# Mixer layer: products of the Fourier and pooling branches moved into the gate groups, the convolution's left behind them

## The chip, the cores and the metric

One core of one Trainium2 chip runs one program that holds a recurrent block, a mixture of experts and two dense layers. The metric is the device time of that program in microseconds (us). Three runs gave 2937.89, 2939.16 and 2935.10 us, so the median is 2937.89 us.

## The reference, cut to what matters

The change lies in the mixer of the dense layers, which runs twice (`l` = 0, 1). With `h` of 512 tokens x 1024 features:

```python
p = h @ w_in[l]                                  # 1024 -> 5 x 512 + 3 x 1024
gates = sigmoid(p[..., OFF_G:]).reshape(b, s, 3, 1024)
y_f = fourier_mix(p[..., F], w_fourier[l])       # 4 groups of 128 -> 256 each
y_c = short_conv(p[..., B], p[..., C], p[..., V], w_conv[l], w_conv_out[l])   # 512 -> 1024
y_p = pool_mix(p[..., P], w_pool[l], pool_scale[l])   # 4 groups (windows 2, 4, 8, 16), 128 -> 256 each
merged = gates[:, :, 0] * y_f + gates[:, :, 1] * y_c + gates[:, :, 2] * y_p
x = x + merged @ w_o[l]
```

Everything is float32. Each matrix product is done as three float32r products of split operands: high part x high part, high x low, low x high.

## The kernel before, in words

Features lie on partitions: a tile is 128 features x 512 tokens, and the model's 1024 features are eight tiles `j` = 0 to 7. The helper `mm3` (L237 to L241) issues the three matmuls of a product: L239 with the high parts, L240 with the input's low part, L241 with the weights' low part.

**Weights.** The class `Stream` reads all weights in the order of their use. A block of 128 x 2048 (1 MB) comes in two halves of 1024 columns; ACT makes the high part `whi` of a half (L190) and DVE the low part `wlo` (L191), into a ring of five halves. `advance(h)`, called when PE's matmuls of half `h` have been issued, splits the next half, so that four halves lie ahead, and `_dma` issues loads as soon as a buffer is free in program order. Loads go through SyncE's queue (SP, L156). The buffers are two `raw`, and inside a section of the layer one `rawf` and one `rawg` (half a block).

**Gate groups.** Four output tiles at a time are computed by `group` in seven steps of 24 matmuls of 256 columns each, with sums of weight blocks. For those sums a pair of weight blocks is loaded as three blocks, of which the first and the third (in `rawg`) get a second load that adds (L154), issued by POOL's queue, since it accumulates. DVE adds two more sums (L196). A group so has seven halves of weights. Its results leave PSUM by six DVE operations (L1603 to L1608, L1626) and copies of ACT.

**Jobs.** Beside the groups, work of earlier groups runs as generators (`jobs`). `tick` at the end of each step runs the next piece of each job, before that step's `advance`; `steps(s3=[...])` starts a job in step 3.

The mixer's groups: the Fourier input, then `c0`, the transform over time, `c1`, `b` and `p` (convolution and pooling inputs), then six gate groups `n` = 0 to 5. Before the change these hold the pooling gates of tiles 0 to 3 and 4 to 7, and four groups with the gates of convolution and Fourier for two tiles each (1, 2, 3, 0). `store` (L1786) takes the sigmoid of a group's results on ACT and writes them to DRAM (`keep`, called `gates` in the trace) through SyncE; only the last group's stay on chip. The split branches go to DRAM as well (`aside`, L1713, `branch` in the trace), and `back` (L1804) reads one branch of a group again, high and low half of 256 KB each, through POOL's queue; `load` (L1827) reads a gate. On chip the groups' split inputs hold 28 of the 40 buffers `s`, and the convolution's result `BC` holds 8.

**The tail of the mixer** (L1849 to L1873). For each tile `j`: four products of the convolution, one of the Fourier branch and one of the pooling branch (18 matmuls of 512 columns), then on DVE gate times product (L1860), two more products (L1862, L1864), two sums (L1863, L1865), on ACT the high part of the merged tile (L1867) and on DVE its low part (L1868), which runs in the next tile's `tick`. Two halves of `w_o` are used on the way (`begin`, behind `j` = 4 and 6), the other six behind the loop (`out_part`).

Of the kernel before, what the change touches and what calls it, by code (L numbers as in the profile page):

```python
# [10 lines left out]
F32 = mybir.dt.float32  # L11
F32R = mybir.dt.float32r
# [9 lines left out]
S = 512  # L22
# [11 lines left out]
JO = (0, 4, 1, 5, 2, 6, 3, 7)  # L34

MIX_OUT = [(j, range(4)) for j in JO[:4]] + [(j, range(4, 7)) for j in JO[:4]] + [(j, (7,)) for j in JO[:4]]
MIX_OUT += [(j, range(8)) for j in JO[4:]]
L2 = 2
# [30 lines left out]
MIX = [((0, 2), (1, 3)), ((8, 12), (9, 13)), ((10, 14), (11, 15)), ((4, 6), (5, 7)), ((16, 18), (17, 19))]  # L69
MIX += [((36 + 4 * i, 38 + 4 * i), (37 + 4 * i, 39 + 4 * i)) for i in range(2)]  # L70
MIX += [((28 + 2 * i, 20 + 2 * i), (29 + 2 * i, 21 + 2 * i)) for i in (1, 2, 3, 0)]


class Stream:
# [35 lines left out]
    def add(self, items, keep=()):  # L110


        self.keep = set(keep)
        self.used = set()
        for it in items:
            if not isinstance(it, tuple):
# [12 lines left out]
            self._ent(a, 0, (a, 1))  # L129
            self._ent(c, 0)  # L130
            self._ent(a, 1)
# [31 lines left out]
    def _src(self, b, half):  # L163
        return self.raw[b][:, half * HB:(half + 1) * HB]

# [7 lines left out]
    def _split(self, late=None):  # L173
# [8 lines left out]
        if b in self.keep:  # L182
            self.half[h] = src
            return True
        hi = self.pool.tile([128, HB], F32R, name="whi", tag="whi", bufs=self.nh)
        lo = self.pool.tile([128, HB], F32R, name="wlo", tag="wlo", bufs=self.nh)
        self.half[h] = (hi, lo)
# [56 lines left out]
def build(tc, A):  # L244
    nc = tc.nc
    ctx = ExitStack()
    with ctx:
# [21 lines left out]
        YD = DR_.tile([S * 2, D], F32, name="YD")  # L269
        keep = [DR_.tile([24, 128, S], F32, name=f"gates{l}") for l in range(L2)]  # L270
        keep_s = [DR_.tile([16, 128, S], F32, name=f"branch{l}") for l in range(L2)]
# [984 lines left out]
def dense_phase(K):  # L1256
# [157 lines left out]

    def out_part(x, done, nxt=lambda j: None, tail=None, order=None, ps=None):

        nonlocal h
        n = 0
        ps = ps or {}
        for j, ks in order or out_order(len(x)):  # L1420
            if tail and j == KD - 1:
# [166 lines left out]
    def mixer(l, nxt):  # L1588
# [58 lines left out]

        def split(src):

            hi, lo = slot(), slot()  # L1650
# [57 lines left out]

        def aside(n, src):

            t = yield from split(src)
            for i in range(2):
                nc.sync.dma_start(keep_s[2 * n + i], t[i].bitcast(F32))  # L1713
# [37 lines left out]

        def pool(t, i):
            half = 1 << i
# [19 lines left out]
            yield  # L1773
            yield from aside(4 + i, t)

# [9 lines left out]

        def store(t, f, n, i):  # L1786

# [4 lines left out]
            for r in range(2):  # L1792
                if n < 5:
                    o = 4 * i + r + 16 if n < 2 else 2 * (2 * i + r)
                    d = keep[o:o + 3:2] if n < 2 else keep[o:o + 2]
                    nc.sync.dma_start(d.rearrange("m p x -> p m x"), t[r].rearrange("p (m x) -> p m x", m=2))
                    yield
                else:
                    G[r] = t[r][:, :S], t[r][:, S:]

# [5 lines left out]

        FT, PL, GP = {}, {}, {}
        new = dict(s0=[once(f3)], s1=[pool(p[0], 0)], s4=[pool(p[1], 1)])
        for n, i in enumerate((0, 1, 1, 2, 3, 0)):
            if n == 5:  # L1810
                FT[0], PL[0] = back(0), back(4)
                v = lines()
                for j in range(2):
                    GP[j] = v[:, j, :S]
                    nc.gpsimd.dma_start(GP[j], keep[16 + j])
            t, f = rows(steps(**new))
            new = dict(s0=[store(t, f, n, i)])
            if n == 0:
                new["s0"].append(pool(p[0], 2))
                new["s3"] = [pool(p[1], 3)]  # L1820
        tick(new["s0"])
        tick()
        assert not jobs

        def load(n):
# [3 lines left out]

        M, PO = [], {}  # L1830

        def begin(js):

            nonlocal h
            w = st.get(h)
            for n, j in enumerate(js):
                PO[j] = bank()
                for k in range(4):
                    sl = slice((4 * n + k) * 128, (4 * n + k + 1) * 128)
                    mm3(nc, PO[j], (w[0][:, sl], w[1][:, sl]), M[k], k == 0, False)  # L1840
            st.advance(h)
            h += 1

        for j in range(KD):
            g = j // 2
            if j % 2 == 0 and j + 2 < KD:
                FT[g + 1], PL[g + 1] = back(g + 1), back(5 + g)
                for i in (j + 2, j + 3):
                    G[i] = load(2 * i), load(2 * i + 1)  # L1849
                    GP[i] = load(16 + i)  # L1850
            gc, gf = G[j]
            gp = GP[j]
            w = st.get(h)
# [15 lines left out]
            if j == 4:  # L1869
                begin(JO[:2])  # L1870
            if j == 6:
                begin(JO[2:4])
        tick()  # L1873
# [4 lines left out]
        open_ffn(3 * l + 2)  # L1878
        out_part(M, done, nxt, order=MIX_OUT[4:], ps=PO)

# [97 lines left out]
def layout(I):  # L1978
# [63 lines left out]
    for e in range(NE):  # L2042
# [4 lines left out]
        [np.asarray(I["moe_w_group"])[0], np.asarray(I["moe_w_expert"])[0]], 1).reshape(KD, 128, 36).transpose(1, 0, 2))  # L2047
    A["rbias"] = np.concatenate([np.asarray(I["moe_b_group"])[0], np.asarray(I["moe_b_expert"])[0]])[None]
    for l in range(L2):
        W = {n: np.asarray(I[n + "_2"])[l] for n in ("w1_a", "w3_a", "w2_a", "w_in", "w_fourier", "w_conv_out",  # L2050
# [25 lines left out]
        tco = tiles(W["w_conv_out"])  # L2076
        hv = []
        for j in range(KD):
            g, r = divmod(j, 2)
            sl = slice(128 * r, 128 * r + 128)  # L2080
            misc = np.zeros((128, 8, 128), f)
            misc[:, 0:4] = tco[j]
            misc[:, 4] = W["w_fourier"][g][:, sl]
            misc[:, 5] = W["w_pool"][g][:, sl]
            hv.append(misc)
        t2 = tiles(W["w_o"])
        ho = list(np.stack([t2[j, :, k] for j, ks in MIX_OUT for k in ks])
                  .reshape(-1, 8, 128, 128).transpose(0, 2, 1, 3))
        hv[5:] = ho[:1] + hv[5:7] + ho[1:2] + hv[7:] + ho[2:]
        put(np.stack([np.ascontiguousarray(v).reshape(128, HB) for v in hv]))  # L2090
# [17 lines left out]
    A["edge"] = ed  # L2108
    A["wblocks"] = np.concatenate(blocks)
    return A  # L2110

# [14 lines left out]
```

## Time and profile before

| | |
|---|---|
| median of three runs | 2937.89 us |
| the profiled execution | 2939.49 us, span 2937.3 us |
| busy share of the span | PE 97%, DVE 76%, ACT 57%, POOL 14% |
| chain that ended last | PE 67%, DVE 9%, ACT 4%, DMA 1% |
| HBM | 557.75 MB read, 33.03 MB written |

A row of the chain or of the time order names engine, line, operation and tiles (out<-in). `[1.68 <-DVE L L1864]` behind a row says that the engine was idle for 1.68 us before it and that the DVE operation of line L1864 ended that. PE's matmuls are pipelined: the time from one start to the next is what one costs, not the duration beside it.

### The profile page before, as it was taken

What the parts mean: (1) busy time and instruction counts of PE and PEld (TensorE: products, weight loads), DVE (VectorE), ACT (ScalarE), POOL (GpSimd) and SP (SyncE); (2) the same over time, 40 slices, a digit from 0 to 9 for tenths busy, and PEclk for the clock granted to TensorE, in tenths of its full rate; (3) what the DMA queues carried; (4) which work ended last, traced back from release to release, by engine and by line L of the source; (5) the groups of instructions that cost most, each with busy time, mean ns of one, the idle gap of its engine ahead of it and who ended that gap; (6) DMA issues with size and microseconds to landing.
All of it is one profiled execution on the core that took longest, in us unless ns stands there. A gap on an engine that the chain in (4) does not pass through costs nothing.

```text
span 2937.3 us, 44478 instructions
## 1 busy us (share of the span) xinstructions
PE 2838.0 (97%) x17882; PEld 2466.9 (84%) x17882; DVE 2239.8 (76%) x2778; ACT 1660.6 (57%) x2214; POOL 421.1 (14%) x395
## 2 busy tenths in 40 slices
PE   9997999999889999999989999999999999899998
PEld 7875666667558989899969999899898999699997
DVE  7688888898986858789678667777587896786674
ACT  4756888888764535655536344644356555363443
POOL 0034222220520000100210000100001002100002
PEclk9998999999999999999999999999999999999999
DMA  6374898999943545478944555465464689445552
GB/s 198 124 279 158 336 361 344 370 365 378 351 161 115 144 136 169 126 192 243 290 153 133 160 162 147 130 179 144 137 176 120 194 242 295 148 139 154 162 144 72
DMA packets 118433, 589.72 MB, mean 201 GB/s; under 512 B 13692, under 2 KB 24316, under 8 KB 65360
## 3 DMA queue, kind: packets, MB, share of 16 engines
q1 hardware_dynamic: 90160, 493.70, 46.2%
q0 software_dynamic: 26976, 92.11, 15.3%
q8 instruction: 141, 2.31, 0.3%
q10 hardware_dynamic: 1088, 1.05, 0.1%
q14 instruction: 68, 0.56, 0.1%
HBM read 557.75 MB, written 33.03 MB: 201 GB/s over the span
## 4 chain that ended last, share of the span: by engine, by line
PE 67%; DVE 9%; ACT 4%; issue 2%; DMA 1%; POOL 0%; DVEq 0%; POOLq 0%; ACTq 0%
PE mm L240 12%; PE mm L241 12%; PE mm L239 12%; PE sv L239 8%; PE sv L241 8%; PE sv L240 8%; DVE wlo L191 4%; ACT whi L190 2%; PE y L949 2%; PE h L914 2%; PE h L913 1%; PE ht L927 1%; DMA raw<-in_wblocks 1%; DVE raw L196 1%; PE gat L884 1%
## 5 line engine op out<-in xcount | busy, mean ns | idle before, releaser
L191 DVE TENSOR_TENSOR wlo<-raw,whi 128x1024 fp32r<-128x1024 f32 x501 | 615.1, 1239 | 199.4 <-ACT whi L190 199.0
L240 PE MATMUL mm<-s,whi 128*128 128x256 f32 (+1 forms) x2246 | 734.2, 327 | 9.6 <-DVE s L1868 9.6
L239 PE MATMUL mm<-s,whi 128*128 128x256 f32 (+1 forms) x2246 | 734.1, 327 | 7.5 <-ACT s L1867 5.3
L241 PE MATMUL mm<-s,wlo 128*128 128x256 f32 (+1 forms) x2246 | 733.4, 327 | 0.0
L190 ACT ACTIVATE whi<-raw 128x1024 fp32r<-128x1024 f32 x503 | 520.1, 1050 | 128.8 <-PE mm L240 88.4
L239 PE MATMUL sv<-s,whi 128*128 128x256 f32 (+1 forms) x1928 | 553.0, 287 | 9.6 <-DVE L L1864 4.1
L240 PE MATMUL sv<-s,whi 128*128 128x256 f32 (+1 forms) x1928 | 551.8, 286 | 0.0
L241 PE MATMUL sv<-s,wlo 128*128 128x256 f32 (+1 forms) x1928 | 551.8, 286 | 0.0
L240 PEld LDWEIGHTS mm<-s,whi 128*128 128x128 f32 x2246 | 425.6, 189 | 50.2 <-DVE s L1868 11.5
L239 PEld LDWEIGHTS mm<-s,whi 128*128 128x128 f32 x2246 | 426.0, 190 | 47.2 <-ACT s L1867 6.1
L241 PEld LDWEIGHTS mm<-s,wlo 128*128 128x128 f32 x2246 | 425.7, 190 | 38.1
L239 PEld LDWEIGHTS sv<-s,whi 128*128 128x128 f32 x1928 | 364.5, 189 | 15.5 <-DVE L L1864 5.3
L241 PEld LDWEIGHTS sv<-s,wlo 128*128 128x128 f32 x1928 | 364.5, 189 | 2.9
L240 PEld LDWEIGHTS sv<-s,whi 128*128 128x128 f32 x1928 | 364.3, 189 | 2.6
L191 DVE TENSOR_TENSOR wlo<-rawf,whi 128x1024 fp32r<-128x1024 f32 x158 | 194.3, 1230 | 69.1 <-ACT whi L190 69.1
L191 DVE TENSOR_TENSOR wlo<-rawb,whi 128x1024 fp32r<-128x1024 f32 x162 | 203.7, 1299 | 22.8 <-ACT whi L190 20.5
L1585 DVE SCALAR_TENSOR_TENSOR X<-mm,X 128x512 f32<-128x512 f32 x95 | 65.6, 691 | 188.1 <-PE mm L241 188.1
L190 ACT ACTIVATE whi<-rawf 128x1024 fp32r<-128x1024 f32 x158 | 166.0, 1050 | 69.3 <-PE mm L240 46.7
L914 PE MATMUL h<-wlo,xt 128*64 128x512 f32 x512 | 195.9, 403 | 6.7 <-DVE wlo L191 5.8
L154 POOL DMA_DIRECT2D rawg<-in_wblocks x63 | 54.6, 867 | 944.3 <-DVE wlo L191 512.2
L913 PE MATMUL h<-whi,xt 128*128 128x512 f32 x448 | 181.6, 405 | 6.0 <-PEq L1125 5.2
L949 PE MATMUL y<-whi,hd 128*64 128x512 f32 x512 | 161.7, 397 | 2.5 <-ACT whi L190 1.5
(459 smaller groups left out, 4696.7 us busy)
## 6 DMA issues: line engine op xcount, KB each, us to landing
raw<-in_wblocks SPq DMA_DIRECT2D x201, 1024.0 KB, 5.3
rawb<-in_wblocks SPq DMA_DIRECT2D x81, 1024.0 KB, 6.8
rawf<-in_wblocks SPq DMA_DIRECT2D x64, 1024.0 KB, 5.1
rawa<-in_wblocks SPq DMA_DIRECT2D x57, 1024.0 KB, 6.8
rawg<-in_wblocks SPq DMA_DIRECT2D x63, 512.0 KB, 3.7
rawg<-in_wblocks POOLq DMA_DIRECT2D x63, 512.0 KB, 6.9
raw<-in_wblocks POOLq DMA_DIRECT2D x48, 512.0 KB, 5.6
gates<-T SPq DMA_DIRECT2D x20, 512.0 KB, 6.7
```

The lines of the kernel that those rows point to most:

```text
L154: self.nc.gpsimd.dma_start(t[:, x:y], src, accum_op=OP.add)
L190: self.nc.scalar.activation(hi, src, AF.Copy)
L191: f = lambda E=self.nc.vector: E.tensor_tensor(lo, src, hi, op=OP.subtract)
L196: f = lambda E=self.nc.vector: E.tensor_tensor(t, t, u, op=OP.add)
L239: nc.tensor.matmul(ps, wh, xh, start=first, stop=False, skip_group_check=skip)
L240: nc.tensor.matmul(ps, wh, xl, start=False, stop=False, skip_group_check=skip)
L241: nc.tensor.matmul(ps, wl, xh, start=False, stop=last, skip_group_check=skip)
L884: nc.tensor.matmul(ps[:, 256 * v:256 * v + 256], x[c][:, sl], K["oh", g][0][:, c], start=c == 0, stop=c == 3)
L913: nc.tensor.matmul(ps, x, w[0][:, sl], start=k == 0, stop=False)
L914: nc.tensor.matmul(ps[:64], x[:, 0:64], w[1][:, sl], start=False, stop=False)
L949: nc.tensor.matmul(ps[i][:64], hd[:, f, v:v + 64], w[wv][:, sl], start=f == 0 and n == 0, stop=f == 3 and n == 2)
L1585: STT(X[j], ps, 0.5, X[j], op0=OP.mult, op1=OP.add)
```

## The change

The order of the gate groups, the place of two of three branch products, and the layout of their weights change. What is computed stays.

- Gate group `n` = 0 now has the convolution's gates of tiles 4 to 7 (stored). Groups 1 to 4 have the gates of pooling and Fourier for the two tiles of one branch group `g` = 2, 3, 0, 1. Group 5 has the convolution's gates of tiles 0 to 3 (kept).
- The products of the branches of `g` stand at the end of its gate group: 12 matmuls of 512 columns into four banks, from a narrow weight block (`wbranch`, 128 x 512) that is loaded through SyncE into a buffer of the ring `t`. The branch's halves are read back by POOL in step 3 of the same group.
- During the next group `gates_pf` multiplies gates and products and adds the two (6 DVE operations a group). The sums `Z` of `g` = 0, 1 stay on chip, those of `g` = 2, 3 go to DRAM and are loaded later.
- Pooling 2 and 3 run beside `n` = 0 and 1, pooling 0 beside 1, pooling 1 beside 2.
- The loop behind the groups has the convolution's product, one multiplication and one addition for each tile; its weights come two tiles to a half. `w_o` stands wholly behind the loop, in the order of `out_order`.

```diff
+MIX += [((32, 34), (33, 35))]
+MIX += [((36 + 2 * i, 20 + 2 * i), (37 + 2 * i, 21 + 2 * i)) for i in (2, 3, 0, 1)]
+MIX += [((28, 30), (29, 31))]
...
-            order += b[:2] + [A["dfts"]] + b[2:]
+            order += b[:2] + [A["dfts"]] + b[2:6]
+            for g in (2, 3, 0, 1):
+                order += [b.pop(6), A["wbranch"][l, g]]
+            order += b[6:]
             sects.append((a, count(order)))
-            order += blocks(8)
+            order += blocks(6)
...
+        if i in (1, 4):
+            st.slots_from(p, "t", 1, lo, hi, bufs=NT_F, w=S)
...
+        def gates_pf(t, f, g, ps):
+
+            f()
+            act(t[0], t[0], AF.Sigmoid)
+            yield
+            act(t[1], t[1], AF.Sigmoid)
+            yield
+            for r in range(2):
+                yield
+                j = 2 * g + r
+                u, v = t[r][:, :S], t[r][:, S:]
+                STT(u, ps[2 * r], vc("pscale", KD * l + j), u, op0=OP.mult, op1=OP.mult)
+                TT(v, v, ps[2 * r + 1], op=OP.mult)
+                if g < 2:
+                    if r == 0:
+                        Z["t"] = lines()
+                    Z[j] = Z["t"][:, r, :S]
+                    TT(Z[j], u, v, op=OP.add)
+                else:
+                    z = tmp()
+                    TT(z, u, v, op=OP.add)
+                    nc.sync.dma_start(keep[8 + j], z)
+                yield
...
+        def branches(g):
+            BR[0], BR[1] = back(4 + g), back(g)
...
+        new = dict(s0=[once(f3), pool(p[0], 2)], s3=[pool(p[1], 3)])
+        for n, g in enumerate((4, 2, 3, 0, 1, 5)):
+            if g < 4:
+                new["s3"] = [once(lambda: branches(g))]
+                if n < 3:
+                    new["s1"] = [pool(p[n - 1], n - 1, spare)]
+            if g == 5:
+                loads(4)
+                loads(5)
+            t, f = rows(steps(**new))
+            if g >= 4:
+                new = dict(s0=[gates_c(t, f, 5 - g)])
+                continue
             w = st.get(h)
-            for n, j in enumerate(js):
-                PO[j] = bank()
-                for k in range(4):
...
+            ps = [bank() for _ in range(4)]
+            for i in range(4):
+                sl = slice(128 * i, 128 * i + 128)
+                mm3(nc, ps[i], (w[0][:, sl], w[1][:, sl]), BR[i % 2], True, True)
             st.advance(h)
             h += 1
+            new = dict(s0=[gates_pf(t, f, g, ps)])
...
+        loads(6)
+        loads(7)
+        M = []
         for j in range(KD):
...
-            py, pf, pq = bank(), bank(), sbank()
-            chunk(w, BC, py)
-            mm3(nc, pf, (w[0][:, 512:640], w[1][:, 512:640]), FT[g], True, True)
-            mm3(nc, pq, (w[0][:, 640:768], w[1][:, 640:768]), PL[g], True, True)
-            st.advance(h)
-            h += 1
+            gc = G[j]
+            py = bank()
+            chunk(st.get(h), BC, py, t0=4 * (j % 2))
             TT(gc, gc, py, op=OP.mult)
             tick()
-            TT(gf, gf, pf, op=OP.mult)
-            TT(gc, gc, gf, op=OP.add)
-            STT(gp, pq, vc("pscale", KD * l + j), gp, op0=OP.mult, op1=OP.mult)
-            TT(gc, gc, gp, op=OP.add)
+            TT(gc, gc, Z[j], op=OP.add)
+            if j % 2:
+                st.advance(h)
+                h += 1
...
-        out_part(M, done, nxt, order=MIX_OUT[4:], ps=PO)
+        out_part(M, done, nxt)
```

## Rows read from the trace of the kernel before

**Rows 1.** The page: busy time, chain by engine, a DMA issue (us to landing).

```profile
PE 2838.0 (97%) x17882; PEld 2466.9 (84%) x17882; DVE 2239.8 (76%) x2778; ACT 1660.6 (57%) x2214; POOL 421.1 (14%) x395
...
PE 67%; DVE 9%; ACT 4%; issue 2%; DMA 1%; POOL 0%; DVEq 0%; POOLq 0%; ACTq 0%
...
rawg<-in_wblocks SPq DMA_DIRECT2D x63, 512.0 KB, 3.7
```

**Rows 2.** Busy time by stretch (PE, PEld, DVE, ACT, POOL, then PEclk, DMA): groups, tails.

```profile
1372.35:1393.24 20.89, 20.30 (x171) 20.09 (x169) 18.92 (x24) 12.75 (x16) 1.73 (x2) 1.00 0.90 279
1413.40:1433.56 20.16, 20.16 (x171) 20.16 (x169) 14.55 (x16) 11.03 (x13) 4.70 (x8) 1.00 0.87 237
2439.91:2459.84 19.93, 19.93 (x170) 19.93 (x169) 14.52 (x16) 11.04 (x13) 4.12 (x7) 1.00 0.90 247
1453.72:1547.09 93.37, 81.85 (x338) 64.60 (x337) 69.75 (x97) 36.66 (x51) 18.93 (x25) 0.95 0.56 188
1513.62:1547.09 33.47, 33.47 (x145) 27.13 (x144) 26.70 (x41) 18.73 (x30) 9.29 (x7) 1.00 0.57 158
2479.77:2574.22 94.45, 83.56 (x339) 65.79 (x337) 69.75 (x96) 35.94 (x49) 18.50 (x25) 0.93 0.55 188
```

**Rows 3.** Order of time on PE in both tails: start, duration, matmul, [idle before].

```profile
1471.66 0.51 PE L239 MATMUL sv<-s,whi 128*128 128x512 f32 x1 [1.68 <-DVE L L1864]
...
1478.51 0.50 PE L239 MATMUL sv<-s,whi 128*128 128x512 f32 x1 [2.37 <-DVE s L1864]
...
1486.68 0.80 PE L239 MATMUL mm<-s,whi 128*128 128x512 f32 x1 [2.65 <-ACT s L1867]
...
2498.56 0.80 PE L239 MATMUL sv<-s,whi 128*128 128x512 f32 x1 [2.40 <-DVE L L1864]
2499.15 0.63 PE L240 MATMUL sv<-s,whi 128*128 128x512 f32 x1
2499.58 0.63 PE L241 MATMUL sv<-s,wlo 128*128 128x512 f32 x1
```

**Rows 4.** Busy time by stretch, behind two of these waits; PEclk is third from last.

```profile
1478.51:1483.20 4.69, 2.59 (x10) 1.80 (x10) 3.04 (x5) 1.58 (x2) 0.11 (x1) 1.00 0.19 59
2498.56:2501.50 2.94, 2.94 (x7) 2.37 (x8) 1.24 (x2) 1.57 (x2) 1.07 (x2) 0.50 1.00 365
```

**Rows 5.** Order of time on DVE, one tile of layer 0's tail.

```profile
1474.04 1.23 DVE L191 TENSOR_TENSOR wlo<-raw,whi 128x1024 fp32r<-128x1024 f32 x1 [1.71 <-ACT whi L190]
...
1477.71 0.75 DVE L1864 SCALAR_TENSOR_TENSOR s<-sv,vec,s 128x512 f32<-128x512 f32 x1
...
1480.83 1.22 DVE L191 TENSOR_TENSOR wlo<-raw,whi 128x1024 fp32r<-128x1024 f32 x1 [1.65 <-ACT whi L190]
```

**Rows 6.** Order of time on ACT, same tile.

```profile
1479.21 0.63 ACT L1867 ACTIVATE s<-s 128x512 fp32r<-128x512 f32 x1 [5.21 <-DVE s L1865]
1479.75 1.04 ACT L190 ACTIVATE whi<-raw 128x1024 fp32r<-128x1024 f32 x1
```

**Rows 7.** Order of time on POOL in the gate groups of both layers.

```profile
1391.68 0.87 POOL L154 DMA_DIRECT2D rawg<-in_wblocks  x1 [15.91 <-DVE wlo L191]
...
1429.38 0.87 POOL L154 DMA_DIRECT2D rawg<-in_wblocks  x1 [15.39 <-DMA gates<-T]
1429.93 2.51 POOL L1804 DMA_DIRECT2D s<-branch  x4
...
2454.67 0.87 POOL L154 DMA_DIRECT2D rawg<-in_wblocks  x1 [14.89 <-DMA gates<-T]
2455.21 2.52 POOL L1804 DMA_DIRECT2D s<-branch  x4
```

**Rows 8.** Instructions of tile `branch`, in 1429:1433 and in 2454:2458: time to landing.

```profile
DMA to landing us min/median/max: 6.4/6.5/6.8
...
DMA to landing us min/median/max: 6.5/6.8/7.1
```

**Rows 9.** DMA issues in 1422.5:1432.3: count, KB each, median us to landing.

```profile
rawg<-in_wblocks SPq DMA_DIRECT2D x1, 512.0 KB, 5.7
```

More of the change, by code (lines that the diff above doesn't have):

```diff
@@ L34 @@
 JO = (0, 4, 1, 5, 2, 6, 3, 7)
-MIX_OUT = [(j, range(4)) for j in JO[:4]] + [(j, range(4, 7)) for j in JO[:4]] + [(j, (7,)) for j in JO[:4]]
-MIX_OUT += [(j, range(8)) for j in JO[4:]]
 L2 = 2
@@ L69 @@
 MIX = [((0, 2), (1, 3)), ((8, 12), (9, 13)), ((10, 14), (11, 15)), ((4, 6), (5, 7)), ((16, 18), (17, 19))]
-MIX += [((36 + 4 * i, 38 + 4 * i), (37 + 4 * i, 39 + 4 * i)) for i in range(2)]
-MIX += [((28 + 2 * i, 20 + 2 * i), (29 + 2 * i, 21 + 2 * i)) for i in (1, 2, 3, 0)]
+MIX += [((32, 34), (33, 35))]
+MIX += [((36 + 2 * i, 20 + 2 * i), (37 + 2 * i, 21 + 2 * i)) for i in (2, 3, 0, 1)]
+MIX += [((28, 30), (29, 31))]
 class Stream:
@@ L115, in add @@
         for it in items:
+            if not isinstance(it, tuple) and it.shape[-1] == S:
+                self._ent(self._block(S, (0, S, it, False)), 0)
+                continue
             if not isinstance(it, tuple):
@@ L163, in _src @@
     def _src(self, b, half):
-        return self.raw[b][:, half * HB:(half + 1) * HB]
+        w = min(HB, self.blocks[b][0])
+        return self.raw[b][:, half * w:(half + 1) * w]
     def _need(self, h):
@@ L184, in _split @@
             return True
-        hi = self.pool.tile([128, HB], F32R, name="whi", tag="whi", bufs=self.nh)
-        lo = self.pool.tile([128, HB], F32R, name="wlo", tag="wlo", bufs=self.nh)
+        hi = self.pool.tile([128, HB], F32R, name="whi", tag="whi", bufs=self.nh)[:, :src.shape[-1]]
+        lo = self.pool.tile([128, HB], F32R, name="wlo", tag="wlo", bufs=self.nh)[:, :src.shape[-1]]
         self.half[h] = (hi, lo)
@@ L269, in build @@
         YD = DR_.tile([S * 2, D], F32, name="YD")
-        keep = [DR_.tile([24, 128, S], F32, name=f"gates{l}") for l in range(L2)]
+        keep = [DR_.tile([16, 128, S], F32, name=f"gates{l}") for l in range(L2)]
         keep_s = [DR_.tile([16, 128, S], F32, name=f"branch{l}") for l in range(L2)]
@@ L1413, in in_chunk, with out_part @@
         return ps
-    def out_part(x, done, nxt=lambda j: None, tail=None, order=None, ps=None):
+    def out_part(x, done, nxt=lambda j: None, tail=None):
         nonlocal h
         n = 0
-        ps = ps or {}
-        for j, ks in order or out_order(len(x)):
+        ps = {}
+        for j, ks in out_order(len(x)):
             if tail and j == KD - 1:
@@ L1646, in steps, with split @@
             return [lambda i=i: tick(new.get(f"s{i}", ())) for i in range(7)]
-        def split(src):
-            hi, lo = slot(), slot()
+        def split(src, to=None):
+            hi, lo = [(to or slot)() for _ in range(2)]
             act(hi, src, AF.Copy)
@@ L1707, in mixer, with aside @@
         h += 2
-        def aside(n, src):
-            t = yield from split(src)
+        def aside(n, src, to=None):
+            t = yield from split(src, to)
             for i in range(2):
@@ L1750, in bc, with pool @@
             BC[i] = yield from split(t)
-        def pool(t, i):
+        def pool(t, i, to=None):
             half = 1 << i
@@ L1773, in pool @@
             yield
-            yield from aside(4 + i, t)
+            yield from aside(4 + i, t, to)
         def once(f):
@@ L1784, in mixer, with gates_c @@
         G = {}
-        def store(t, f, n, i):
+        Z = {}
+        spare = lambda: line(F32R)[:, :S]
+        def gates_c(t, f, i):
             f()
@@ L1792, in store @@
             for r in range(2):
[L1793 to L1796, printed above, removed]
+                v = t[r].rearrange("p (m x) -> p m x", m=2)
+                if i:
+                    nc.sync.dma_start(keep[4 + r:8:2].rearrange("m p x -> p m x"), v)
                     yield
                 else:
-                    G[r] = t[r][:, :S], t[r][:, S:]
+                    for m in range(2):
+                        G[2 * m + r] = v[:, m]
+        def gates_pf(t, f, g, ps):
[20 more added lines that the diff above has]
+                yield
         def back(n):
@@ L1805, in back @@
             return t
[L1807 to L1823, printed above, removed]
         def load(n):
@@ L1828, in load, with loads @@
             return g
-        M, PO = [], {}
-        def begin(js):
-            nonlocal h
-            w = st.get(h)
-            for n, j in enumerate(js):
-                PO[j] = bank()
-                for k in range(4):
-                    sl = slice((4 * n + k) * 128, (4 * n + k + 1) * 128)
-                    mm3(nc, PO[j], (w[0][:, sl], w[1][:, sl]), M[k], k == 0, False)
+        def loads(j):
+            G[j], Z[j] = load(j), load(8 + j)
+        BR = {}
+        def branches(g):
+            BR[0], BR[1] = back(4 + g), back(g)
@@ L1841, in begin @@
             st.advance(h)
             h += 1
-        for j in range(KD):
[L1845 to L1853, printed above, removed]
-            py, pf, pq = bank(), bank(), sbank()
-            chunk(w, BC, py)
-            mm3(nc, pf, (w[0][:, 512:640], w[1][:, 512:640]), FT[g], True, True)
-            mm3(nc, pq, (w[0][:, 640:768], w[1][:, 640:768]), PL[g], True, True)
-            st.advance(h)
-            h += 1
+            new = dict(s0=[gates_pf(t, f, g, ps)])
@@ L1860, in mixer @@
+        tick(new["s0"])
+        tick()
+        assert not jobs
+        loads(6)
+        loads(7)
+        M = []
+        for j in range(KD):
+            gc = G[j]
+            py = bank()
+            chunk(st.get(h), BC, py, t0=4 * (j % 2))
             TT(gc, gc, py, op=OP.mult)
             tick()
-            TT(gf, gf, pf, op=OP.mult)
-            TT(gc, gc, gf, op=OP.add)
-            STT(gp, pq, vc("pscale", KD * l + j), gp, op0=OP.mult, op1=OP.mult)
-            TT(gc, gc, gp, op=OP.add)
+            TT(gc, gc, Z[j], op=OP.add)
+            if j % 2:
+                st.advance(h)
+                h += 1
@@ L2048, in layout @@
     A["rbias"] = np.concatenate([np.asarray(I["moe_b_group"])[0], np.asarray(I["moe_b_expert"])[0]])[None]
+    wbranch = np.zeros((L2, 4, 128, 4, 128), f)
     for l in range(L2):
@@ L2076, in layout @@
         tco = tiles(W["w_conv_out"])
[L2077 to L2085, printed above, removed]
+        hv = [np.concatenate([tco[j], tco[j + 1]], 1) for j in range(0, KD, 2)]
+        for g in range(4):
+            for r in range(2):
+                for m, n in enumerate(("w_pool", "w_fourier")):
+                    wbranch[l, g, :, 2 * r + m] = W[n][g][:, 128 * r:128 * r + 128]
         t2 = tiles(W["w_o"])
-        ho = list(np.stack([t2[j, :, k] for j, ks in MIX_OUT for k in ks])
-                  .reshape(-1, 8, 128, 128).transpose(0, 2, 1, 3))
-        hv[5:] = ho[:1] + hv[5:7] + ho[1:2] + hv[7:] + ho[2:]
+        hv += list(np.stack([t2[j, :, k] for j, ks in out_order(KD) for k in ks])
+                   .reshape(-1, 8, 128, 128).transpose(0, 2, 1, 3))
         put(np.stack([np.ascontiguousarray(v).reshape(128, HB) for v in hv]))
@@ L2109, in layout @@
     A["wblocks"] = np.concatenate(blocks)
+    A["wbranch"] = wbranch.reshape(L2, 4, 128, S)
     return A
```

5 lines of the change are left out of this document (1 added, 4 removed).

## The prediction

> **What bounds the kernel now.** I read the page first: TensorE (PE) is busy for 97% of the span and 67% of the chain that ended last is PE [rows 1]. So only a stretch in which PE waits can be shortened. The table by stage finds it [rows 2]. A gate group (168 matmuls of 256 columns) takes 20.16 us, with PE busy all of it and the clock at 1.00. Behind the last group stands the tail: 8 x 18 = 144 product matmuls and 8 x 24 = 192 matmuls of `w_o`, all of 512 columns. The last 144 of them run undisturbed in 33.47 us, 0.2324 us each, so all 336 would need 78.1 us. The tail takes 93.37 us in layer 0 and 94.45 us in layer 1: 15.3 + 16.3 = **31.6 us** are lost there. In the order of time on PE one sees where: waits of 1.7 to 2.7 us, ended by the operations that build the merged tiles, and after some of them matmuls that start 0.43 us apart and not 0.23 [rows 3]; the granted clock is 0.50 there, which is 1.2 GHz [rows 4].
>
> Why the tail waits, VectorE (DVE) and ScalarE (ACT) tell [rows 5, 6]. For one `j` DVE runs the weights' low part (1.23 us) and six operations of up to 0.75 us, 5.1 us with the low part (1474.04 to 1479.2), and then idles 1.65 us until ACT has made `hi` of the merged tile (0.63 us) and, behind it in ACT's order, the high part of the next weights (1.04 us). That is 6.8 us a tile, where PE's 18 matmuls need 4.2 us.
>
> **The change, part by part.** PE's work stays the same: 4 groups x 12 product matmuls + 8 x 12 convolution matmuls = 144, of 512 columns as before.
>
> *Removed from the tail.* Per `j` three of the five 512-wide DVE operations go. Left are product, sum with `Z[j]` and low part, about 2.0 us, and per two `j` one weight split of 1.23 us: 5.2 us of DVE for 24 matmuls (5.6 us of PE). The split now stands behind an odd `j` only and ahead of that `j`'s `hi`, so DVE has no ACT chain to wait for. `w_o` starts 8 x 2.8 = 22.3 us behind the last group, with `M[0]` to `M[5]`; the product of `j` = 5 ends at 16.7 us and its low part is due some 4 us later; `M[6]` and `M[7]` are due another 8.4 us later. I let all **31.6 us** go. What is late next there is nothing on PE until the FFN. The conv gates and sums `Z[6]`, `Z[7]` load behind the last group; they have 16.7 us.
>
> *DVE in the groups.* A group with gated sums gets 6 operations of about 0.69 us and one narrow split, 4.8 us. The group from 1413.40 on, without pooling work, has DVE busy 14.55 us; 19.3 us of 22.9 us (20.16 + 12 x 0.2324) fit, and weights are split four halves ahead. The one from 1372.35 on, with pooling work left, had 18.9 us [rows 2]; pooling is now spread over three groups, not two. Cost: nothing on PE, as long as those four halves of lead (11 us) hold.
>
> *Branch reads in the groups: the term that decides.* The 12 matmuls at the end of a group read `BR`, four 256 KB halves, which POOL's queue loads in step 3 of that group. POOL issues in order. Ahead of them stands the accumulating load into `rawg` (next group's third block), which cannot go before SyncE's plain load into `rawg` has landed, which waits for this group's third block to be split in step 1. The trace of before holds this very sequence, since `back(0)` and `back(4)` stand behind the same accumulating load: POOL sits idle 15.4 us, issues `rawg` at 1429.38 and the four `s<-branch` from 1429.93 on, the last one at 1429.93 + 2.51 - 0.87 = 1431.57 [rows 7], though all they read had long been stored. The group began at 1413.40 [rows 2], so that is 16 us into it; the last half lands 6.8 us after its issue [rows 8], at 25.0 us. In layer 1 the group begins at 2439.91 [rows 2], `rawg` goes at 2454.67, and the last half lands at 24.0 us [rows 7, 8]. PE wants the first half at 20.16 us, and 8 of the 12 matmuls (1.9 us) stand behind the last one, where they should all end at 22.95 us. So a wait of landing + 1.9 - 22.95: **3.9 us and 2.9 us** by these rows. Behind the waiting products stands every matmul of the next group.
>
> How far this carries over: SyncE's `rawg` load took 5.7 us there [rows 9], under full DMA load; its median over the kernel is 3.7 us [rows 1]. With that, the wait is about 1.9 us. After the change the load has fewer stores beside it (20 gate stores a layer become 8) and the block that ran beside it is issued later, behind the branch loads' step. For the three later groups of each layer I take 2.5 us, between 1.9 and 3.9: 6 x 2.5 = 15.0 us. The first group with products follows pooling 2 and 3, a place in which `rawg` was late: 1391.68 in a group that began at 1372.35 [rows 2, 7], 19.3 us, so 7.2 us of wait by that row, 1.9 us at the least; I take 5.0: 10.0 us for two layers. Half clock after such waits: after 2.40 us of idling some 7 matmuls ran at 0.43 us (1.4 us lost), after 2.37 us none did [rows 3, 4]. I take 1.5 us for the two long waits and 1 us for all others, 4.0 us; bounds 0 and 8 x 1.5 = 12 us.
>
> A rule weighed against this: the Trainium skill, DMA: Bandwidth & Descriptors, "Anatomy of one DMA — SWDGE (gpsimd) path", gives a transfer from GpSimd's queue about 2.0 us plus its bytes at 436 GB/s. From the `rawg` issue to the landing of the last half (1.5 MB) that would be 5.6 us, as an estimate; the rows show 9.0 and 9.2 us [rows 7, 8], so the trace disagrees. By the rule the later groups would wait 0 to 0.5 us, and the time would be that of the first rival.
>
> *At nothing:* narrow weight blocks (four of 256 KB in place of two of 1 MB a layer) and fewer gate stores lie beside PE; SyncE's wait for a `t` buffer delays blocks that are due half a group later; uncovered, it would add to the waits above.
>
> **Sum**, on the profiled execution's own 2939.5 us (span 2937.3): 2939.5 - 31.6 + 15.0 + 10.0 + 4.0 = 2936.9 us. The median of the runs shown is 1.6 us below the profiled run: **2935 us**.
>
> **Rivals.**
> *The loads land in time* (faster). The wait vanishes where the last half lands by 21.1 us. For it: half the stores go, and the median `rawg` load is 2 us shorter than the one beside those branch loads [rows 1, 9]. Against: even then 1.9 us remain by rows, unless the four loads also land faster than 6.5 us behind the accumulating one. Time: 2937.9 - 31.6 = 2906 us, or about 2916 us if the first group of each layer still waits. The figure of the Trainium skill given above speaks for this case.
> *The waits outgrow the tail* (slower). One mechanism: the branch halves stand behind the `rawg` accumulation in POOL's queue, and there are eight such waits, so it decides at 31.6 / 8 = 3.95 us each, half clock included. By the rows as they stand, 3 x (3.9 + 2.9) + 2 x 7.2 = 34.8 us, and with a clock loss of 1.5 us at each, 46.8 us: 2937.9 + 15.2 = 2953 us. For it: of the three waits by rows one is at this point and one beyond it. Against: a lighter queue.
> *The tail isn't relieved* (the change doesn't do what it says): late loads of `G` and `Z`, or DVE late from the last group, keep half of the 31.6 us: 2935 + 16 = 2951 us. Against: loads took about 6.5 us and have 16.7.
>
> **How the numbers follow.** About 0.2% (5.9 us) is what can be told from no change; so faster is below 2932, slower above 2944. Waits that eat most of the gain: 0.43, with its own range of 2926 to 2944 (0.14 of it faster, 0.02 slower). In time: 0.25. Outgrown: 0.27 (0.03 within 0.2%). Not relieved: 0.05. Faster 0.14 + 0.25 = 0.39; same 0.27 + 0.03 = 0.30; slower 0.02 + 0.24 + 0.05 = 0.31. The range, 2908 to 2952, leaves out about half of the first rival and a fifth of the second.
>
> **What would show it.** In the tail after: no PE wait over 0.3 us, `w_o` starting 22 to 23 us behind the last group, clock 1.00. At the end of the four groups with products: a PE wait that ends with a DMA into `s` from `branch`, 2 to 4 us, longest in the first group of each layer; in POOL's order `rawg` issued 14 to 16 us into the group with the four loads right behind it. The prediction fails if these waits are absent (then about 2906), if they average over 4 us, or if tail waits remain.

## The result and the profile after

The changed kernel takes 2951.53 us (median of 5 runs, 2949.42 to 2956.53) against 2937.44 us for the kernel before in the same comparison (5 runs, 2935.10 to 2939.16). The ratio is 1.0051, with a 95% interval of 1.0036 to 1.0066: slower, by some 14 us, where the forecast's terms came to 2.6 us faster (31.6 gained, 29.0 lost). The time lies just inside the range, 0.5 us below its upper end. The profiled run took 2954.42 us with a span of 2952.6 us, 15.3 us more than before.

The page after, the lines that answer to [rows 1]. PE is still busy for 96%, but the chain now holds DMA with 4%, of which 2% are the branch reads. The row of L241, the first matmul of `mm3`, has 33.6 us of idle time ahead of it, and 31.4 us of that end with a DMA into `s` from `branch`.

```profile
PE 2845.1 (96%) x17882; PEld 2471.1 (84%) x17882; DVE 2230.4 (76%) x2778; ACT 1657.6 (56%) x2214; POOL 403.7 (14%) x371
...
PE 72%; DVE 4%; DMA 4%; ACT 2%; issue 1%; POOL 0%; POOLq 0%; SPq 0%; ACTq 0%; DVEq 0%
...
L241 PE MATMUL mm<-s,whi 128*128 128x256 f32 (+1 forms) x2262 | 744.6, 329 | 33.6 <-DMA s<-branch 31.4
...
rawg<-in_wblocks SPq DMA_DIRECT2D x63, 512.0 KB, 3.6
```

The table by stage after, which answers to [rows 2]; the columns are PE, PEld, DVE, ACT, POOL, PEclk, DMA share, GB/s. Each group (first and third row) has its twelve branch products behind it (second and fourth); the last two rows are the tails' 288 matmuls.

```profile
1384.49:1407.70 23.21, 20.41 (x169) 20.23 (x168) 14.17 (x20) 12.59 (x16) 3.08 (x5) 1.00 0.42 124
1407.70:1415.09 7.39, 5.53 (x13) 3.76 (x14) 7.32 (x9) 0.00 (x0) 0.90 (x1) 0.56 0.93 278
1415.09:1436.83 21.74, 20.25 (x169) 20.06 (x168) 12.44 (x16) 11.66 (x14) 3.06 (x5) 0.99 0.54 157
1436.83:1445.29 8.46, 5.58 (x13) 3.56 (x14) 6.70 (x8) 0.00 (x0) 0.90 (x1) 0.65 0.70 226
...
1493.09:1560.01 66.92, 66.92 (x290) 54.27 (x289) 54.07 (x74) 34.44 (x49) 12.57 (x9) 1.00 0.43 136
2525.40:2592.30 66.90, 66.90 (x290) 54.26 (x289) 53.29 (x74) 34.16 (x49) 12.09 (x9) 1.00 0.43 135
```

The tails run through: 66.9 us for 288 matmuls is 0.2323 us each, PE busy all the time, clock 1.00. The loss has moved to the products. Twelve matmuls that need 2.8 us took 7.39 and 8.46 us, at a mean clock of 0.56 and 0.65, and the stretch ahead of them, which runs to the first product, holds the first wait: 23.21 us, where 168 matmuls take 19.93 us [rows 2].

PE's order of time after, at the reads of five groups: start, duration, matmul, idle time and what ended it. The first row is the first group of layer 0; the row at 2442.62 is layer 1.

```profile
1378.86 0.80 PE L241 MATMUL mm<-s,whi 128*128 128x512 f32 x1 [7.31 <-DMA s<-branch]
...
1407.70 0.47 PE L241 MATMUL mm<-s,whi 128*128 128x512 f32 x1 [2.80 <-DMA s<-branch]
1410.03 0.80 PE L242 MATMUL mm<-s,whi 128*128 128x512 f32 x1 [1.86 <-DMA s<-branch]
...
1436.83 0.47 PE L241 MATMUL mm<-s,whi 128*128 128x512 f32 x1 [1.50 <-DMA s<-branch]
1438.21 0.50 PE L242 MATMUL mm<-s,whi 128*128 128x512 f32 x1 [0.91 <-DMA s<-branch]
...
1440.43 0.80 PE L241 MATMUL mm<-s,whi 128*128 128x512 f32 x1 [1.49 <-DMA s<-branch]
...
1467.73 0.47 PE L241 MATMUL mm<-s,whi 128*128 128x512 f32 x1 [1.96 <-DMA s<-branch]
...
2442.62 0.57 PE L241 MATMUL mm<-s,whi 128*128 128x512 f32 x1 [3.95 <-DMA s<-branch]
```

One group can wait four times, since its products read four halves that land one after the other. Why they land late is in POOL's and SyncE's order of time after, and in the time to landing of the reads issued from 1398.91, from 1429.70 and from 1460.09:

```profile
1398.36 0.89 POOL L155 DMA_DIRECT2D rawg<-in_wblocks  x1 [22.32 <-DVE T L1823]
1398.91 2.53 POOL L1838 DMA_DIRECT2D s<-branch  x4
...
1429.12 0.88 POOL L155 DMA_DIRECT2D rawg<-in_wblocks  x1 [17.51 <-DVE t L1831]
1429.70 2.48 POOL L1838 DMA_DIRECT2D s<-branch  x4
...
1459.50 0.87 POOL L155 DMA_DIRECT2D rawg<-in_wblocks  x1 [16.71 <-DVE L L1828]
...
1399.23 0.38 SPq L157 DMA_DIRECT2D t<-in_wbranch  x1
1399.71 0.48 SPq L157 DMA_DIRECT2D raw<-in_wblocks  x1
...
1431.08 0.67 SPq L157 DMA_DIRECT2D raw<-in_wblocks  x1
...
1457.31 0.33 SPq L157 DMA_DIRECT2D raw<-in_wblocks  x1
...
DMA to landing us min/median/max: 8.7/10.6/10.9
...
DMA to landing us min/median/max: 7.0/8.7/10.3
...
DMA to landing us min/median/max: 7.5/7.7/7.9
```

The accumulating load goes 13.9 us into the group that began at 1384.49 and 14.0 us into the one that began at 1415.09, just as forecast. But within 2 us of it SyncE issues the next group's narrow block and its 1 MB `raw` load. Before, the four reads took 6.4 to 6.8 us to land in layer 0 [rows 8]; now they take up to 10.9 us there, and up to 12.1 us in layer 1. In the last of these groups, in both layers, the 1 MB load goes 2.2 us ahead of the accumulating load (1457.31 and 1459.50); there the reads land after 7.5 to 7.9 us (6.8 to 7.2 in layer 1), and PE idles least, 1.96 and 1.44 us in all.

One gain had not been forecast. Before, the FFN behind each mixer began with waits of its own. PE's two waits there in layer 0 and DVE's order of time, both of the kernel before, and under them the one row of after that answers: the last sum of the mixer (`X` from `mm`).

```profile
1554.12 0.39 PE L239 MATMUL mm<-x,whi 128*128 128x256 f32 x1 [2.60 <-ACT x L1358]
1555.46 0.38 PE L240 MATMUL mm<-x,whi 128*128 128x256 f32 x1 [0.95 <-DVE x L1366]
```

```profile
1547.50 0.68 DVE L1876 TENSOR_TENSOR X<-mm,X 128x512 f32<-128x512 f32 x1
1548.10 1.71 DVE L191 TENSOR_TENSOR wlo<-raw,whi 128x1024 fp32r<-128x1024 f32 x1
1549.85 2.20 DVE L196 TENSOR_TENSOR raw<-raw 128x1024 f32<-128x1024 f32 x1
1551.97 0.68 DVE L1876 TENSOR_TENSOR X<-mm,X 128x512 f32<-128x512 f32 x1
```

```profile
1560.21 0.69 DVE L1897 TENSOR_TENSOR X<-mm,X 128x512 f32<-128x512 f32 x1 [1.09 <-PE mm L243]
```

Before, PE ended the mixer at 1547.09 and the last sum began 4.9 us later, behind 3.9 us of weight work. The old order of `w_o` ends four tiles together, so their sums come to DVE in a bunch. PE's two waits are for tiles made from that sum. After, the tiles end one by one, and the last sum begins 0.2 us behind PE's end (1560.01). I count a stretch's loss as its length from first to last matmul start less 0.1187 us for each 256-column and 0.2324 us for each 512-column matmul. By that the FFN's first step lost 7.59 and 6.64 us before, and 0.85 us each after: 12.5 us gained.

The span's 15.3 us, by the same count: tails -31.6, FFN starts -12.5, branch reads +59.6, smaller waits of the mixer -2.3, everything ahead of the dense layers -0.9, and +3.0 at the program's close, where SyncE waits 3.0 us and not 0.5 us for PE's sequencer. The 59.6 us are 15.8 us of waits in the two first groups, 26.3 us in the six later ones, and 17.5 us of slow matmuls behind them, some 16 us of it at a granted clock of 0.50 (1.2 GHz). In this count a matmul that starts 0.4 us or more late has waited, and a smaller delay makes it a slow one; the page's idle time for the same waits is less, 31.4 us on L241 and 5.4 us on L242.

### The profile page after: what moved, and what is told of

The parts are those of the page before. It is cut to its first block, busy times and chain, and to the rows that moved or that the text cites. A ratio compares the mean times of both kernels' runs of the same rounds, so it can differ in the third digit from the quotient of the medians.

```text
span 2952.6 us, 44425 instructions
## 1 busy us (share of the span) xinstructions
PE 2845.1 (96%) x17882; PEld 2471.1 (84%) x17882; DVE 2230.4 (76%) x2778; ACT 1657.6 (56%) x2214; POOL 403.7 (14%) x371
## 3 DMA queue, kind: packets, MB, share of 16 engines
q0 software_dynamic: 25056, 85.82, 14.6%
## 4 chain that ended last, share of the span: by engine, by line
PE 72%; DVE 4%; DMA 4%; ACT 2%; issue 1%; POOL 0%; POOLq 0%; SPq 0%; ACTq 0%; DVEq 0%
PE mm L242 14%; PE mm L243 14%; PE mm L241 14%; PE sv L241 8%; PE sv L243 8%; PE sv L242 8%; PE y L954 3%; DMA s<-branch 2%; DVE wlo L193 2%; PE h L919 2%; PE h L918 2%; ACT whi L192 1%; PE ht L932 1%; DMA rawg<-in_wblocks 1%; PE gat L889 1%
## 5 line engine op out<-in xcount | busy, mean ns | idle before, releaser
L241 PE MATMUL mm<-s,whi 128*128 128x256 f32 (+1 forms) x2262 | 744.6, 329 | 33.6 <-DMA s<-branch 31.4
L193 DVE TENSOR_TENSOR wlo<-raw,whi 128x1024 fp32r<-128x1024 f32 x493 | 606.7, 1240 | 221.5 <-ACT whi L192 221.4
L242 PE MATMUL mm<-s,whi 128*128 128x256 f32 (+1 forms) x2262 | 745.1, 329 | 5.8 <-DMA s<-branch 5.4
L243 PE MATMUL mm<-s,wlo 128*128 128x256 f32 (+1 forms) x2262 | 742.6, 328 | 0.0
L192 ACT ACTIVATE whi<-raw 128x1024 fp32r<-128x1024 f32 x495 | 513.2, 1051 | 156.5 <-PE mm L242 101.3
L241 PE MATMUL sv<-s,whi 128*128 128x256 f32 (+1 forms) x1912 | 544.3, 285 | 1.7 <-ACT sv L1486 1.7
L242 PE MATMUL sv<-s,whi 128*128 128x256 f32 (+1 forms) x1912 | 543.6, 284 | 0.0
L243 PE MATMUL sv<-s,wlo 128*128 128x256 f32 (+1 forms) x1912 | 543.5, 284 | 0.0
L241 PEld LDWEIGHTS mm<-s,whi 128*128 128x128 f32 x2262 | 430.4, 190 | 77.4 <-DMA s<-branch 18.8
L242 PEld LDWEIGHTS mm<-s,whi 128*128 128x128 f32 x2262 | 430.4, 190 | 51.9 <-DMA s<-branch 12.0
L241 PEld LDWEIGHTS sv<-s,whi 128*128 128x128 f32 x1912 | 359.9, 188 | 4.5 <-ACT sv L1486 2.3
L242 PEld LDWEIGHTS sv<-s,whi 128*128 128x128 f32 x1912 | 360.0, 188 | 2.1
L193 DVE TENSOR_TENSOR wlo<-rawb,whi 128x1024 fp32r<-128x1024 f32 x162 | 200.1, 1276 | 22.4 <-ACT whi L192 20.3
L1486 ACT ACTIVATE sv<-mm 128x512 f32<-128x512 f32 x63 | 36.6, 582 | 249.2 <-PE mm L243 249.1
```

The costliest lines, as they stand in the source:

```text
L192: self.nc.scalar.activation(hi, src, AF.Copy)
L193: f = lambda E=self.nc.vector: E.tensor_tensor(lo, src, hi, op=OP.subtract)
L241: nc.tensor.matmul(ps, wh, xh, start=first, stop=False, skip_group_check=skip)
L242: nc.tensor.matmul(ps, wh, xl, start=False, stop=False, skip_group_check=skip)
L243: nc.tensor.matmul(ps, wl, xh, start=False, stop=last, skip_group_check=skip)
L1486: act(pv, pm, AF.Copy)
```

## The experiments

The theory: the branch reads stand behind the accumulating load in POOL's queue and, beside the 1 MB weight load, land too late. Each experiment was timed against the kernel before on the same chip; ratios are to that kernel. Starting the reads in step 2 was not run: it gives the same instructions with the same waits, in the same order on every engine, as step 3. Only a step ahead of the accumulating load's place changes POOL's order.

**1. Reads in step 0**, ahead of the accumulating load into `rawg`:

```diff
-                new["s3"] = [once(lambda: branches(g))]
+                new["s0"].append(once(lambda: branches(g)))
```

> The four branch reads of a group are issued in its step 0 and not in step 3, so that they stand ahead of the accumulating rawg load in POOL's queue; nothing else changes. Theory (place in POOL's queue: the reads wait some 14 us for the rawg load, and then land 10 to 13 us later): the reads are issued within 3 us of the group's start and land before 16 us, the waits at the products of groups 2 to 4 vanish, the first group's shrink or stay at up to 8 us, since its buffers come free from pooling 3 some 15 us into it: 2893 to 2908 us. Rival (bandwidth: the reads, 1 MB, have no room beside the weights anywhere in the group, or hold up the weights instead): over 2935 us, with PE waiting for weights or for the reads.

Measured: 2907.98 us, ratio 0.9891 (0.9875 to 0.9908), at the upper end of what the theory gave. No later group waits for its reads. What is left is 13.2 us in the two first groups, half clock included. POOL's, SyncE's and PE's order of time in this kernel show why:

```profile
1367.37 0.54 POOL L1838 DMA_DIRECT2D s<-branch  x1 [8.67 <-DVE wlo L193]
1368.16 0.54 POOL L1838 DMA_DIRECT2D s<-branch  x1 [0.25 <-issue]
...
1359.72 0.90 SPq L1720 DMA_DIRECT2D branch<-s  x2
...
1374.71 0.51 PE L241 MATMUL mm<-s,whi 128*128 128x512 f32 x1 [2.08 <-DMA s<-branch]
```

Two of the four reads go only when pooling 3's stores, issued at 1359.72 and landed at 1366.8 and 1367.6, give their `s` buffers back. The profile names DVE as the releaser of the first, but each of the two follows the landing of one store by 0.5 us, and experiment 6, which starts pooling 3 a step earlier, bears it out.

**2. Reads through SyncE's queue**, still in step 3:

```diff
-                nc.gpsimd.dma_start(t[i].bitcast(F32), keep_s[2 * n + i])
+                nc.sync.dma_start(t[i].bitcast(F32), keep_s[2 * n + i])
```

> The branch reads stay in step 3 but go through SyncE's queue, and so no longer stand behind the rawg accumulation; every read of a branch is issued ahead of that step's narrow weight block and 1 MB raw block. Theory (place in POOL's queue): issued 12 to 14 us into the group, landed by 21 us, waits of 0 to 2 us: 2893 to 2912 us. Rival (bandwidth beside the 1 MB raw load decides): they land as late as through POOL, waits of 4 to 7 us stay: over 2930 us.

Measured: 2917.82 us, 0.9923 (0.9906 to 0.994), 6 us above the theory's range and well below the rival's. The waits shrink but do not go. On SyncE the reads stand behind a gate store that waits for DVE, so they go 14.6 and 14.0 us into the second and third group with products of layer 0, no earlier than on POOL; but now they are ahead of SyncE's `raw` load, and land 2.8 to 7.0 us behind their issue. In the fourth group that load came first, as these rows of SyncE's order of time show, and there the reads took 6.8 to 9.8 us:

```profile
1437.96 0.33 SPq L157 DMA_DIRECT2D raw<-in_wblocks  x1
1438.38 2.63 SPq L1838 DMA_DIRECT2D s<-branch  x4
```

So two things make the reads late: the moment of issue, and what is issued beside them. Experiment 1, with 7, takes the first by itself, experiment 5 the second.

**3. No reads**:

```diff
-            BR[0], BR[1] = back(4 + g), back(g)
+            BR[0], BR[1] = BC[0], BC[1]
```

> The four reads of a group are left out and its products take two tiles that lie on chip (the branches' values are not used, so the output is another). Theory (the waits for these reads are the whole loss): the 59 us that the groups gained over their matmuls go, 2892 us within 4. Rival (products in the groups cost by themselves, by PSUM banks or by DVE falling behind with the gated sums): waits stay at the group ends, over 2915 us.

Measured: 2895.09 us, 0.9851 (0.9834 to 0.9867), within what the theory gave. From 1384 to 1500 us PE is busy for 115.67 of 116.00 us, clock 1.00. So the whole slowdown hangs on these reads; without their waits the change would have gained 44 us, about the tails' 31.6 and the FFN starts' 12.5 us.

**4. The old order of `w_o`** in the changed kernel, where four tiles end together (`WO` is also the order in which the weights are laid out):

```diff
+WO = [(j, range(7)) for j in JO[:4]] + [(j, (7,)) for j in JO[:4]] + [(j, range(8)) for j in JO[4:]]
...
-        out_part(M, done, nxt)
+        out_part(M, done, nxt, order=WO)
```

> The changed kernel, with the output projection's tiles in an order like that of before: the first four tiles end together, the last four one by one. Theory (the two FFN starts gained some 5 us each because the tiles now end one by one, so that DVE isn't behind with sums and splits when the last one ends): the start of the FFN behind both mixers has again PE waits of 2.5 to 4 us and 1 us, 2961 us within 4. Rival (the FFN starts gained by the lighter transfers or by the clock): no change, 2951 us.

Measured: 2970.93 us, 1.0102 (1.0085 to 1.0118). The FFN starts lose 7.94 and 7.78 us again, 14.0 us more than in the changed kernel, where 10 were expected; the mechanism is shown, its size was put too low. DVE's order of time has the pattern of before: the last sum behind 3.9 us of weight work.

```profile
1562.43 0.68 DVE L1898 TENSOR_TENSOR X<-mm,X 128x512 f32<-128x512 f32 x1
1563.04 1.72 DVE L194 TENSOR_TENSOR wlo<-rawf,whi 128x1024 fp32r<-128x1024 f32 x1
1564.79 2.18 DVE L199 TENSOR_TENSOR rawf<-rawf 128x1024 f32<-128x1024 f32 x1
1566.89 0.68 DVE L1898 TENSOR_TENSOR X<-mm,X 128x512 f32<-128x512 f32 x1
```

**5. The 1 MB load held back** from step 3 to step 5:

```diff
         def branches(g):
             BR[0], BR[1] = back(4 + g), back(g)
+            st.gate = st.nb + 1
...
                 new["s3"] = [once(lambda: branches(g))]
+                new["s5"] = [once(lambda: setattr(st, "gate", 1 << 30))]
```

> The changed kernel, with the next group's 512-column weight load (1 MB on SP's queue) held back from step 3 to step 5 of a group, so that it is not issued beside the branch reads. In the changed kernel that load is issued within 1 us of the accumulating load's trigger, and the last of the four reads lands 10.1 to 13.1 us behind that trigger, where before it landed 9.0 us behind. Theory (the 1 MB load shares the 16 DMA engines with the reads and stretches them): the reads land about 9 us behind the trigger, the later groups wait 2 to 3 us each as the prediction had it, and the time falls by some 15 to 25 us of the 59.6 us of waits, to about 2930 us (2925 to 2937). Rival (the accumulating load and GpSimd's queue alone set the landing): still 10 to 13 us, the same waits, about 2951 us. A second rival: the weight load itself now comes late and the wait goes from the reads to the high halves; then more than 2951 us.

Measured: 2946.85 us, 1.0031 (1.0019 to 1.0042): slower than expected by 17 us, and its interval overlaps that of the changed kernel (1.0036 to 1.0066) a little, so the time alone tells little. The trace says which half of the theory held. POOL's and SyncE's order of time, the landing of the four reads from 1401.16, and the page's row:

```profile
1400.60 0.89 POOL L155 DMA_DIRECT2D rawg<-in_wblocks  x1 [16.50 <-DVE T L1823]
1401.16 2.54 POOL L1838 DMA_DIRECT2D s<-branch  x4
...
1410.33 0.44 SPq L157 DMA_DIRECT2D raw<-in_wblocks  x1
...
DMA to landing us min/median/max: 7.5/7.7/7.8
...
L241 PE MATMUL mm<-s,whi 128*128 128x256 f32 (+1 forms) x2262 | 743.7, 329 | 26.9 <-DMA s<-branch 22.9
...
1373.01 0.50 SPq L157 DMA_DIRECT2D raw<-in_wblocks  x1
```

The load moves in four of the six later groups; in the last of each layer it still goes ahead of the accumulating load. In the four the last half lands 9.2 to 11.0 us behind the accumulating load's trigger (its issue on POOL), not 12.4 to 14.3, and their waits fall from 22.0 to 10.6 us. The other two land after 9.8 and 10.2 us (10.1 and 9.4 in the changed kernel) and wait about as before. The six wait 15.4 us in all (26.3 in the changed kernel), near the 15.0 us of the forecast. Two things ate the rest. In the first group the holding back put the load beside the reads rather than 6 us ahead of them (1373.01; 1365.40 in the changed kernel), and there the last half landed 9.5 us behind its issue instead of 7.9; the first groups' waits rose from 15.8 to 20.3 us. And the slow matmuls behind the shorter waits still cost 16.4 us, about what they cost in the changed kernel; I had expected them to shrink with the waits.

**6. Reads in step 0 and pooling 3 one step earlier**:

```diff
-        new = dict(s0=[once(f3), pool(p[0], 2)], s3=[pool(p[1], 3)])
+        new = dict(s0=[once(f3), pool(p[0], 2)], s2=[pool(p[1], 3)])
...
-                new["s3"] = [once(lambda: branches(g))]
+                new["s0"].append(once(lambda: branches(g)))
```

> The kernel with the branch reads in step 0 (2908.0 us, ratio 0.989 to before), and pooling 3 of the first group started in step 2 rather than step 3. Theory: the excess of 5.0 + 6.3 us and the half clock of 1.1 + 0.8 us that stayed at the first groups is there because the third and fourth read wait for the buffers that pooling 3's stores set free (stores issued at 1359.7, landed 1366.8; reads issued 1367.4 and 1368.2); a step earlier, about 3 us of time, the reads go 3 us sooner and the first groups lose 5 to 10 us in all: about 2900 us (2897 to 2904). Rival (the reads of the first group wait for something else in GpSimd's queue, such as the accumulating load): no change, 2908 us.

Measured: 2897.47 us, 0.9861 (0.9844 to 0.9877), within the theory's range and 2.4 us from the kernel without reads. The first groups have no wait left. This is the fastest full version, 1.4% below the kernel before.

**7. Reads in step 1**, two steps earlier:

```diff
-                new["s3"] = [once(lambda: branches(g))]
+                new["s1"] = [once(lambda: branches(g))]
                 if n < 3:
-                    new["s1"] = [pool(p[n - 1], n - 1, spare)]
+                    new["s1"].append(pool(p[n - 1], n - 1, spare))
```

> The changed kernel with the branch reads two steps earlier, in step 1 of the group. The instruction streams of PE, DVE, ACT and SP stay as they are; on POOL alone the four reads change places with one instruction, the accumulating load into rawg, which now stands behind them. Theory (the place behind that one load is what makes the later groups wait: 26.3 us of PE's waits and 12.9 us at half clock behind them): the reads of the later groups go out 8 to 14 us earlier, land before the group ends, and those waits vanish; the first group of each layer still waits, as with the reads in step 0, for buffers that pooling 3's stores set free (6.1 and 7.1 us with half clock there). Time about 2951.5 - 39.2 - (20.4 - 13.2) = 2905 us, 2902 to 2912. Rival (whoever stands second pays: the accumulating load behind the reads now brings the next group's third weight block late, and PE waits for weights): more than 2920 us, with waits at the weights' high halves.

Measured: 2907.43 us, 0.9893 (0.9877 to 0.991), within the theory's range. But this is no new variant: it gives the same instructions with the same waits, in the same order on every engine, as experiment 1. So it is experiment 1 measured once more, and that the two times agree (0.9891 and 0.9893) shows how well a time repeats, not more of the cause. POOL's order of time here and in experiment 1, where the reads follow the accumulating load into `raw` at once, ahead of `rawg`, and the page's row here:

```profile
1403.78 0.89 POOL L155 DMA_DIRECT2D raw<-in_wblocks  x1 [9.41 <-DVE T L1611]
1404.34 2.53 POOL L1838 DMA_DIRECT2D s<-branch  x4
1417.66 0.89 POOL L155 DMA_DIRECT2D rawg<-in_wblocks  x1 [10.80 <-DVE wlo L193]
...
1405.37 0.89 POOL L155 DMA_DIRECT2D raw<-in_wblocks  x1 [10.01 <-DVE T L1611]
1405.92 2.53 POOL L1838 DMA_DIRECT2D s<-branch  x4
1420.10 0.89 POOL L155 DMA_DIRECT2D rawg<-in_wblocks  x1 [11.65 <-DMA rawg<-in_wblocks]
...
L241 PE MATMUL mm<-s,whi 128*128 128x256 f32 (+1 forms) x2262 | 738.6, 327 | 6.8 <-DMA s<-branch 4.0
```

One exchange on one queue takes PE's 31.4 us of waits for the reads on L241 down to 4.0, and the time down by some 44 us. What is left is 10.4 us in the two first groups, for the buffers of experiment 1, whose trace had 13.2 us; by so much two traces of one program differ in this count. The weight load that is now second makes nobody late.

## Why the prediction was wrong

*The tail* (-31.6 us): right to the tenth. No wait, clock 1.00, and `w_o` 96 x 0.2323 = 22.3 us behind the last group.

*The place of the wait*: right. `rawg` goes 13.9 to 14.2 us into the later groups of layer 0 and 19.3 us into its first (the forecast: 14 to 16, and 19.3 by the row), the four reads right behind it, and the longest wait in the first group. Experiment 3 shows that PE waits there for these reads alone, experiments 1 and 7, one program measured twice, that this queue order is the cause.

*The step that failed* is the size of that wait, in the prediction's words "the block that ran beside it is issued later, behind the branch loads' step", counted as a relief. It was issued later: into the reads' own time. Six later groups at 2.5 us were to cost 15.0 us and cost 26.3. Of these, 22.0 us fell on the four where the 1 MB load was issued 0.5 to 2.0 us behind the accumulating load; the two where it went ahead cost 2.2 us each, near the forecast. Two first groups at 5.0 us were to cost 10.0 and cost 15.8. For the first groups the row had said 7.2 us each; I had taken a value between it and the lower bound, and the row itself was nearly right (7.3 and 7.2 us of idling on the trace, 7.9 us each by the count used here). The prediction's own sign of failing came true: the eight waits average 5.3 us, over 4. Experiment 5 moves that one load out of the four groups' way and their waits halve, and where it moves the load into the way, in the first groups, the wait grows. "Lighter queue" was an average over the layer; what counts is what is issued within 2 us of the reads.

*Half clock* (4.0 us): 17.5 us of slow matmuls. I priced it by the stall's length from two stalls of the tail. Here the twelve products of layer 0's later groups run at a mean of 0.56, 0.65 and 0.72 of the full clock. In two of these groups PE stops two and four times within a few us, but a single wait of 1.96 us had 0.72 behind it, where one of 1.97 us in experiment 5 had 1.00. So the length of a stall was no measure of its price; what sets it stays open. My upper bound, 12 us, was too low as well.

*The missing term* (-12.5 us): the order of `w_o` changed too, which I read as part of the tail and did not follow into the FFN. With the old order (experiment 4) the changed kernel is 1.0% slower than before, not 0.5%.

*The rival that happened* is "the waits outgrow the tail". It named the mechanism and decided at 3.95 us for each of eight waits; they came to 59.6 / 8 = 7.5 us. Its 2953 us is near the 2951.5 us measured only since two misses cancel: 12.8 us more of waits and half clock than its 46.8, and the 12.5 us of the FFN.

*The rule weighed*: for the 1.5 MB from the trigger to the last landing, taken as one transfer, the Trainium skill, DMA: Bandwidth & Descriptors, "Anatomy of one DMA — SWDGE (gpsimd) path", gives an estimate of 5.6 us. The runs show 9.4 to 14.3 us in the later groups of the changed kernel and 9.2 to 11.0 in experiment 5, so the trace disagrees more than before. The Trainium skill, Trainium Kernel Development and Optimization, "Key Constraints", says that DMAs from the SP, ACT and POOL queues share the same 16 engines and interleave; experiment 5 agrees (7.8 us to landing, not 10.9, once SyncE's load is elsewhere), and by that rule the question would have been which other queue's loads meet the reads.

## What to carry to other kernels

In this case a load that an engine waited for was priced by its place in its queue and by what the other queue issued in the same 2 us, not by the mean load; so list both for the moment of issue in the new order, since a moved step carries the loads behind it along. Put such a read ahead of an accumulating load that itself waits, then look for the buffer it needs. And a change of order in one stage is followed to the first matmul of the next.

## What the runs showed of the hardware

- The last read landed 9.0 and 9.2 us behind the accumulating load's trigger before. In the later groups of the changed kernel it took 12.4 to 14.3 us where a 1 MB load was issued on another queue 0.5 to 2.0 us behind that trigger, and 9.4 and 10.1 us where that load was issued 2.2 us ahead of it. In experiment 5, with the load held back in the first four, it took 9.2 to 11.0 us there.
- The granted clock behind a wait did not follow the wait's length. Behind single waits of 1.96 us (changed kernel, 1467.73), 1.97 us (experiment 5, 1408.77) and 1.44 us (experiment 5, 1461.24) the twelve products ran at mean clocks of 0.72, 1.00 and 0.67; behind 7.2 us of idling in layer 1 (changed kernel, 2412.65) at 0.50 throughout.
- At the program's close SyncE waited 3.0 us for PE's sequencer in the changed kernel and in experiments 1, 4, 5, 6 and 7, but 0.5 us before and 0.7 us in experiments 2 and 3. The cause stays open; some 2.3 us of each difference in time between these two sets may come from there.
